# A hybrid encoder step: moving two sets of loads to ScalarE's queue and fixing the order of some products on TensorE

## The chip, the core and the metric

The kernel runs on one core of a Trainium2 chip. A core has five engines that run side by side, each with its own stream of instructions: TensorE multiplies matrices (PE in the profile, PEld for its loads of the stationary operand), VectorE (DVE) and GpSimd (POOL) work elementwise, ScalarE (ACT) computes functions and copies, and SyncE (SP) issues transfers. A transfer (DMA) can be issued from the stream of SP or of ScalarE; the profile names these queues q1 and q10. An engine takes its instructions in the order of its stream: one that must wait holds up all that stand behind it on that engine.

The metric is the device time of one execution in microseconds (us).

## The reference, cut to what matters

The reference computes one inference step of a two-layer encoder, for 2048 prompt tokens and 32 sampled tokens (2080 rows, model width 1024), all in float32.

Layer A is a gated delta rule with 8 heads of 128. The input is multiplied with a weight matrix of 4096 columns (and 16 for the gates). The columns of q, k and v pass a short causal convolution; then, in blocks, a state S per head is read and updated:

```python
decay = jnp.exp(jnp.where(incl, gcum[..., :, None] - gcum[..., None, :], -jnp.inf))
lower = jnp.where(strict, jnp.einsum('nbhik,nbhjk->nbhij', kbeta, kc) * decay, 0.0)
...
v_new = ui - jnp.einsum('bhck,bhkv->bhcv', wi, s)
o = jnp.einsum('bhck,bhkv->bhcv', qd, s) + jnp.einsum('bhij,bhjv->bhiv', ai, v_new)
s = s * gl[..., None, None] + jnp.einsum('bhck,bhcv->bhkv', kd, v_new)
```

The output o is normalized, weighed with a gate z, multiplied with output weights, added to the input and layer-normalized: this is h. From h come the shared keys and values, the queries and the gates of layer B, which is attention over a sliding window, again with output weights and a layer norm.

## The kernel before, in words

Products in float32 are made of three products of rounded parts: each operand is split into a high part (hi, a cast on ScalarE) and the rest (lo, a subtraction), and hi·hi, hi·lo and lo·hi are summed in PSUM. Tokens are taken in five blocks of 416 for projections and in 17 tiles of 128 (the last one holds the 32 sampled tokens) elsewhere. The kernel runs in stages:

1. **Projection** (class P1, `qkv`). For each of 24 columns of 128 outputs, weights are loaded (L46) and split (L53, L54), multiplied with the five blocks (`project`, L77 to L79), copied from PSUM into a row R by ScalarE (L258), convolved (L198 on ScalarE, three sums at L200 on VectorE), passed through tanh (L203) and stored. From column 7 on, one part of the output weights per column is loaded, split and stored again (`split_out_weights`, L1033 to L1036), in a buffer of the tag that tanh uses as well. From column 16 on, `decays` (L220) makes four or five decay matrices E per column: it loads cumulated gates, broadcast over 128 partitions (L231), adds a mask on VectorE (L239), takes the exponential on ScalarE (L243) and stores E (L244). E has three buffers; the load is made two steps ahead of its use. All of this is free for the planner: the framework simulates the program and sends each instruction when it is ready in the simulation, the earlier in the program the sooner.
2. **Gates z** of the first three blocks, beside first inverses.
3. **Delta stage** (class Delta, `run`). Seventeen chunks (the sampled one first) pass through a software pipeline. The string ORDER has 91 steps with offsets; each of the iterations i goes through all of them, for chunk i + offset. The engines TensorE, VectorE and ScalarE keep this written order here (`manual_schedule`); SP and GpSimd do not. In an iteration, `Lk` loads k, `G0` and `G1` multiply it (L627), `tv` transposes v (L741), `sp` and `SU` update the state, `oa` makes o, `sq`, `X`, `R` and `OSC` normalize it, and `otr`, `z`, `st` transpose it (L848), weigh it (L852) and store it (L855). From iteration OPEN = 11 on, the left part of the memory is free, and a function `side` is called after the steps 30 and 60: each call takes a step of `load_whole_weights`, two loads of 512 KB, high and low part (L1045, L1046), eight in all. From the ninth call on, the tables of the layer norm are loaded. From the last two iterations on, `second.give(0.45)` after each step with products fills in a group of output products (`OutNorm.tile`, L1070 to L1072, six products each). After the loop come the sampled tokens' last transposes, with 2 us of filling after each half.
4. **Output A** (class O1). What is left of the output products runs through `second.rest()`, in written order on TensorE and VectorE. Each tile is normalized (to L1148), stored, transposed (L1175), copied and stored again as hT.
5. **Layer B** (class P2, then Attention). `open_left` (called at L1661) loads the blocks 2 to 4 of hT and splits them (L68, L69); gate 1 is multiplied with the blocks 0 and 1 (L1662), then the gates 0 and 1 with the blocks 2 to 4, then values, keys, queries and attention. None of it has a written order.

Of the kernel before, what the change touches and what calls it, by code (L numbers as in the profile page):

```python
# [10 lines left out]
F32 = mybir.dt.float32  # L11
# [23 lines left out]
def new_pool(tc, es, name, bufs=1, space=None, side=None):  # L35
    kw = {"reuse_waits": "tile"}
    if side is not None:
        kw["side"] = side
    if space is not None:
        kw["space"] = space  # L40
    return es.enter_context(tc.tile_pool(name=name, bufs=bufs, **kw))
# [49 lines left out]
def drain(gen):  # L91
    for _ in gen:
        pass


class P1:
# [123 lines left out]
    def decays(self):  # L220

        nc, G, T = self.nc, self.G, self.T
        nm = self.one.tile([128, 128], F32, tag="triu", name="nm")
        nc.sync.dma_start(nm[:], self.I["nm"])
        todo = [(t, q) for t in (NTT - 1, *range(NTT - 1)) for q in range(2)]

        def load(m):
            t, q = todo[m]
            n, hs = min(128, NT - t * 128), slice(q * 4, q * 4 + 4)
            E = self.one.tile([128, 4, 128], F32, tag=("parts", "sel", "gtmp")[m % 3], name="E")  # L230
            nc.sync.dma_start(E[:, :, :n], T["gcum"][t, hs, :n].partition_broadcast(128))  # L231
            return E, t, n, hs

        ahead = [load(0), load(1)]
        for m in range(len(todo)):
            E, t, n, hs = ahead.pop(0)
            if m + 2 < len(todo):
                ahead.append(load(m + 2))
            nc.vector.tensor_tensor(out=E[:n, :, :n], in0=E[:n, :, :n],  # L239
                                    in1=nm[:n, :n].unsqueeze(1).to_broadcast([n, 4, n]), op=ALU.add)  # L240
            for j in range(4):
                h = hs.start + j
                nc.scalar.activation(E[:n, j, :n], E[:n, j, :n], AF.Exp, bias=G["ngc"][:n, t, h:h + 1])  # L243
            nc.scalar.dma_start(T["E"][t, :n, hs, :n], E[:n, :, :n])  # L244
            yield
# [291 lines left out]
class Delta:  # L537
# [365 lines left out]
    def run(self, chunks, S, gate, second, side, done):  # L903


        order = [(t[:t.index("+")], int(t[t.index("+") + 1:])) for t in self.ORDER.split()]
        steps, last = self.steps(), len(chunks) - 1
        for c, ch in enumerate(chunks):
            ch.S, ch.last = (self.S if ch.pool is None else S), ch.pool is not None or c == last
        gate.plan(order, self.FIRST + 2, self.WHOLE)  # L910
        gate.begin()
        for i in range(self.FIRST, last + 4):
            if i == self.OPEN:
                gate.finish()
                side(None)
            for p, (name, off) in enumerate(order):
                c = i + off
                if name in gate.STEPS:
                    m = c + gate.shift
                    gate.step(name, m)  # L920
                elif 0 <= c <= last and self.wanted(chunks[c], name):
                    steps[name](chunks[c])
                    if i >= last - 1 and name in self.WORK:
                        second.give(0.45)
                    if name == "st1":
                        done(chunks[c])
                if i >= self.OPEN and p in (len(order) // 3, 2 * len(order) // 3):
                    side(True)
            if i == last - 3 or i == last - 2:
                next(second.gen)  # L930
        c0 = chunks[0]
        c0.o = self.four.tile([128, 8, 128], F32, tag="gb", name="os", bufs=1)
        self.nc.sync.dma_start(c0.o[:NS], self.T["o"][:, :, :])
        self.load(c0, "z")
        for q in range(2):
            self.back(c0, q)
            self.gated(c0, q)
            self.store(c0, q)
            second.give(2.0)
        done(c0)  # L940

    def sampled(self, pool):
# [97 lines left out]
def load_whole_weights(nc, pool, kept):  # L1040

    hi, lo = (pool.tile([128, KC, D], F32R, tag=n, name=n) for n in ("wo_hi", "wo_lo"))
    yield hi, lo
    for k in range(KC):
        nc.sync.dma_start(hi[:, k, :].bitcast(F32), kept[0, k])  # L1045
        nc.sync.dma_start(lo[:, k, :].bitcast(F32), kept[1, k])  # L1046
        yield


# [542 lines left out]
def program(tc, I, O, T, G):  # L1592
    nc = tc.nc
    left, right, mid = ExitStack(), ExitStack(), ExitStack()
    p1 = P1(tc, left, right, mid, I, O, T, G)
    p1.qkv()
    mid.close()
    zp = new_pool(tc, left, "p1_z", 2, side="left")
    chunks = [Chunk(NP, NS)] + [Chunk(t * 128, 128) for t in range(16)]
    chunks[0].pool = zp  # L1600
    ahead = Ahead(tc, mid, left, I, O, T, G).inverses(chunks[:2])
    next(ahead)
    w = p1.first_gate(nc.gpsimd)
    z = p1.z((0, 1, 2), zp, ("zth", "z"), p1.ps, nc.gpsimd, w)
    with tc.manual_schedule(engines={mybir.EngineType.PE, mybir.EngineType.DVE}):
        for _ in range(28):
            next(z)
        for i, _ in enumerate(ahead):
            if i < 8 or i % 2:
                next(z, None)  # L1610
        drain(z)
    w = p1.first_gate(nc.gpsimd)
    raw = p1.late_raw(zp, 1)
    mid.close()
    right.close()
    delta = Delta(tc, right, I, O, T, G)
    S = delta.sampled(zp)
    sent = set()
    o1 = []

    def side(o):
        if o is None:
            left.close()
            o1.append(O1(tc, left, I, O, T, G))
        else:
            next(o1[0].on.rest, None)
            if o1[0].steps == 8:
                o1[0].on.tabs = o1[0].on.tables()
            o1[0].steps += 1

    def outputs():
        tiles = [(t * 128, t * 128, min(128, NT - t * 128)) for t in range(NTT)]
        yield from o1[0].tiles(tiles, lambda t: t[0] in sent, more)

    def more(i):
        if i == 0:
            p2[0].load_right()
            for j in range(2):
                p2[0].slab(j, nc.gpsimd)
        else:  # L1640
            yield from p2[0].gate(0, (i - 1,), p2[0].ps)

    p2 = []
    second = Filler(outputs())

    def done(ch):
        sent.add(ch.t0)

    ET = mybir.EngineType
    with tc.manual_schedule(engines={ET.PE, ET.DVE, ET.Activation}):  # L1650
        delta.run(chunks, S, LateGate(p1, zp, w, raw), second, side, done)
    right.close()
    hp = new_pool(tc, right, "o1_hT", 1, side="right")
    o1[0].room = lambda: hp.tile([128, KC, 128], F32, tag="hT", name="hT")
    p2.append(P2(tc, right, I, O, T))
    o1[0].bank = p2[0].ps
    with tc.manual_schedule(engines={ET.PE, ET.DVE}):
        second.rest()
    left.close()
    p2 = p2[0]  # L1660
    p2.open_left(left)  # L1661
    drain(p2.gate(1, (0, 1), p2.ps))  # L1662
    for b in (2, 3, 4):
        for i in (0, 1):
            drain(p2.gate(i, (b,), p2.ps))
    p2.values()
    p2.rotated()
    for i in (2, 3):
        p2.slab(i, nc.gpsimd)
        drain(p2.gate(i, range(NB), p2.ps))  # L1670
    late = range(4, 8)
    for i in late:
        p2.slab(i, nc.gpsimd)
        drain(p2.gate(i, (2, 3, 4), p2.ps))
    left.close()
    att = Attention(tc, left, I, O, T, G)
    att.load_kv(12, 18)
    order = list(range(14, 32)) + list(range(14))
    for i in late:
        p2.slab(i, nc.vector)  # L1680
        drain(p2.gate(i, (0, 1), p2.right_ps))
        att.chunk(order.pop(0))
        if i == late[0]:
            att.load_kv(18, 32)
    right.close()
    att.open_right(right)
    att.load_kv(0, 12)
    for n in order:
        for _ in range(2):
            next(att.rest, None)  # L1690
        att.chunk(n)
        if n == order[-2]:
            att.sample()
            att.flush(2)
        elif n % 2 == 1 and n != order[-1]:
            att.flush(3 if n < 24 and n > 13 else 2)
    att.flush(0)
    left.close()
    right.close()
# [138 lines left out]
```

## Time and profile before

| | us |
|---|---|
| three runs | 2221.84, 2222.75, 2215.28 (median 2221.84) |
| the profiled execution | 2216.86 |
| its span, from the first to the last instruction | 2215.1 |
| TensorE busy in it | 2150.1 |
| ScalarE busy | 901.1 |
| VectorE busy | 1379.1 |

All rows of the trace are from the profiled execution, in us from the start of its span; it took 1.8 us more than its span. A row of the timeline gives the start, the duration, the engine (SPq or ACTq for an issue of a transfer), the line, the instruction, what it writes and reads, the shape and, in brackets, how long the engine stood idle before it and what ended the wait. A row of waits gives who waited for whom, the sum, how often, and the longest. A row of windows gives a stretch, its length, the busy time of each engine with its number of instructions, the clock granted to TensorE as a share of full speed, the share of time that the 16 DMA engines were busy, and the GB/s that they moved. By their position in the trace, the stages are: the projection up to about 600, the delta stage up to about 1170, output A up to about 1355, layer B from there.

### The profile page before, as it was taken

The page shows a single profiled execution, that of the slowest core. Times are in us where ns is not written, and L with a number is a line of the kernel's source. Part 1 is how long each engine was busy: PE and PEld are TensorE (multiplying, and loading weights), DVE is VectorE, ACT ScalarE, POOL GpSimd, SP SyncE. Part 2 cuts the span into 40 slices and gives each one's busy share as a digit, 9 for nine tenths or more (in the row PEclk, how much of TensorE's full clock was granted, in tenths as well). Part 3 has the DMA queues.
Part 4 walks back from the last instruction along what each step waited for, and adds up shares of the span by engine and source line. Part 5 has one row for each costly group of instructions (what it writes and reads, how often), then busy time and mean ns, then how long its engine had stood idle before and what let it go on. Part 6 is the DMA issues. An engine that isn't in the chain of part 4 may idle for free.

```text
span 2215.1 us, 36944 instructions
## 1 busy us (share of the span) xinstructions
PE 2150.1 (97%) x13690; PEld 1980.3 (89%) x13690; DVE 1379.1 (62%) x2701; ACT 901.1 (41%) x2274; POOL 826.3 (37%) x1201
## 2 busy tenths in 40 slices
PE   8999999999899999996989999999999999999998
PEld 6999999999899999996977887999999987778885
DVE  3676666665567688885866886224543235668775
ACT  4444444456522566665641213222111245544442
POOL 1422223212212377776630201035442124555564
PEclk9999999999999999998999999999999999999999
DMA  5223333357655454448425764355212287233321
GB/s 196 68 61 90 99 111 106 97 170 223 192 157 157 145 161 160 152 157 324 160 85 184 231 196 125 125 197 187 83 66 79 73 196 264 77 93 98 96 72 53
DMA packets 268116, 308.29 MB, mean 139 GB/s; under 512 B 79728, under 2 KB 198832, under 8 KB 267664
## 3 DMA queue, kind: packets, MB, share of 16 engines
q1 hardware_dynamic: 253664, 285.42, 41.2%
q10 hardware_dynamic: 14272, 20.51, 2.7%
q8 instruction: 108, 1.77, 0.3%
q14 instruction: 72, 0.59, 0.1%
HBM read 189.63 MB, written 116.60 MB: 138 GB/s over the span
## 4 chain that ended last, share of the span: by engine, by line
PE 83%; DMA 7%; DVE 4%; POOL 2%; ACT 2%; issue 1%; SPq 0%; ACTq 0%; DVEq 0%; POOLq 0%
PE ps L77 14%; PE ps L79 14%; PE ps L78 14%; PE po L1070 5%; PE po L1072 5%; PE po L1071 5%; PE ot L1562 4%; DMA E<-s_gcum 2%; PE S L1541 2%; PE tr L1556 2%; DMA s_E<-E 1%; PE g L627 1%; PE gq L754 1%; PE sp L769 1%; PE ks L769 1%
## 5 line engine op out<-in xcount | busy, mean ns | idle before, releaser
L77 PE MATMUL ps<-act_hi,w_hi 128*128 128x416 f32 x2000 | 707.7, 355 | 5.9 <-ACT R L258 2.4
L79 PE MATMUL ps<-act_hi,w_lo 128*128 128x416 f32 x2000 | 706.5, 354 | 4.3 <-POOL w_lo L54 2.1
L78 PE MATMUL ps<-act_lo,w_hi 128*128 128x416 f32 x2000 | 703.2, 352 | 3.5 <-DVE act_lo L69 3.5
L77 PEld LDWEIGHTS ps<-act_hi,w_hi 128*128 128x128 f32 x2000 | 377.4, 189 | 12.8 <-ACT act_hi L68 3.7
L79 PEld LDWEIGHTS ps<-act_hi,w_lo 128*128 128x128 f32 x2000 | 376.8, 188 | 10.5 <-POOL w_lo L54 3.1
L78 PEld LDWEIGHTS ps<-act_lo,w_hi 128*128 128x128 f32 x2000 | 377.0, 188 | 9.7 <-DVE act_lo L69 5.3
L54 POOL TENSOR_TENSOR w_lo<-w_raw,w_hi 128x1024 fp32r<-128x1024 f32 x44 | 117.7, 2675 | 473.4 <-ACT w_hi L53 446.2
L200 DVE SCALAR_TENSOR_TENSOR y<-R,convw,y 128x2083 f32<-128x2083 f32 x72 | 181.8, 2526 | 38.7 <-POOL convo L194 22.5
L661 POOL TENSOR_TENSOR tm<-L,Tt 128x60 f32<-128x60 f32 (+19 forms) x375 | 130.3, 347 | 116.6 <-DVE tm L661 48.0
L1549 POOL TENSOR_TENSOR P<-P,sm 128x384 f32<-128x384 f32 (+2 forms) x128 | 100.6, 808 | 169.7 <-DVE sm L1427 101.2
L663 POOL TENSOR_TENSOR Tt<-Tt,tm 128x60 f32<-128x60 f32 (+19 forms) x375 | 143.8, 383 | 29.4
L1423 ACT ACTIVATE P<-S,nm 128x192 f32<-128x192 f32 (+3 forms) x260 | 104.8, 419 | 90.5 <-DVE nm L1416 43.8
L258 ACT COPY R<-ps 128x416 f32<-128x416 f32 (+1 forms) x144 | 60.7, 444 | 123.8 <-PE ps L79 105.3
L1070 PE MATMUL po<-wo_hi,g_hi 128*128 128x512 f32 x256 | 104.6, 408 | 0.0
L1072 PE MATMUL po<-wo_hi,g_lo 128*128 128x512 f32 x256 | 101.2, 395 | 0.5 <-DVE g_lo L1113 0.5
L1071 PE MATMUL po<-wo_lo,g_hi 128*128 128x512 f32 x256 | 100.9, 394 | 0.0
L1267 POOL TENSOR_TENSOR rs<-rs,sin 128x416 f32<-128x416 f32 x50 | 70.7, 1414 | 78.1 <-DVE rs L1266 72.3
L53 ACT CAST w_hi<-w_raw 128x1024 fp32r<-128x1024 f32 x48 | 50.4, 1050 | 119.5 <-PE ps L78 82.7
L1562 PE MATMUL ot<-pt,vd 128*128 128x256 f32 x372 | 97.1, 387 | 1.6 <-ACT pt L1558 1.1
L1070 PE MATMUL po<-wo,g_hi 128*128 128x512 f32 x224 | 92.9, 415 | 0.0
L1352 DVE SCALAR_TENSOR_TENSOR za<-zs,za 128x416 f32<-128x416 f32 x40 | 33.0, 826 | 93.3 <-ACT za L1351 93.2
L1072 PE MATMUL po<-wo,g_lo 128*128 128x512 f32 x224 | 90.1, 402 | 0.0
(301 smaller groups left out, 4073.6 us busy)
## 6 DMA issues: line engine op xcount, KB each, us to landing
w_raw<-in_w_in SPq DMA_DIRECT2D x40, 512.0 KB
w_raw<-in_b_w_in SPq DMA_DIRECT2D x20, 512.0 KB
k<-s_k SPq DMA_DIRECT2D x17, 512.0 KB
E<-s_E SPq DMA_DIRECT2D x17, 512.0 KB
s_bz<-za SPq DMA_DIRECT2D x40, 208.0 KB
s_bq<-ra SPq DMA_DIRECT2D x40, 208.0 KB
s_q<-y SPq DMA_DIRECT2D x8, 1024.0 KB
s_wo<-wo_parts SPq DMA_DIRECT2D x16, 512.0 KB
```

Of the source, the lines that this page charges most:

```text
L54: sub.tensor_tensor(out=lo[:], in0=raw[:], in1=hi[:], op=ALU.subtract)
L77: nc.tensor.matmul(ps, hi[:, k, :], xh[:, k, :], start=(k == 0), stop=False)
L78: nc.tensor.matmul(ps, hi[:, k, :], xl[:, k, :], start=False, stop=False)
L79: nc.tensor.matmul(ps, lo[:, k, :], xh[:, k, :], start=False, stop=(k == KC - 1))
L200: nc.vector.scalar_tensor_tensor(out=y[:], in0=R[:, j:j + W], scalar=self.convw[:, i, j:j + 1], in1=y[:], op0=ALU.mult, op1=ALU.add)
L661: P.tensor_tensor(out=tm[:n, i0 - k:, :w], in0=L[:n, i0:, j:j + 1].to_broadcast(sh), in1=Tt[:n, j:j + 1, :w].to_broadcast(sh), op=ALU.mult)
L663: P.tensor_tensor(out=Tt[:n, i0:, :w], in0=Tt[:n, i0:, :w], in1=tm[:n, i0 - k:, :w], op=ALU.subtract)
L1070: nc.tensor.matmul(ps[:n], ghi[:, k, :n], w[0][:, k, cs], start=a, stop=False)
L1071: nc.tensor.matmul(ps[:n], ghi[:, k, :n], w[1][:, k, cs], start=False, stop=False)
L1072: nc.tensor.matmul(ps[:n], glo[:, k, :n], w[0][:, k, cs], start=False, stop=z)
L1423: nc.scalar.activation(P[u], src, AF.Exp, bias=nm[:, u:u + 1], scale=1.0, accum_out=sm[:, u:u + 1])
L1562: nc.tensor.matmul(ot[:, p], self.vd[:, kc0 + j, p, :], pt[:, 2 * j:2 * j + 2, :], start=(j == 0), stop=(j == nj - 1))
```

## The change

It has four parts.

1. The loads of the output weights (L1045, L1046) are issued from ScalarE instead of SP, and `load_whole_weights` gives a step back after each single load. `side` is called in each iteration from OPEN on at the positions p with p % 18 = 10, that is 10, 28, 46, 64 and 82 of 91. The tables follow at the seventeenth call.
2. The loads of decays (L231) are issued from ScalarE, one step ahead instead of two.
3. The sampled tokens' last transposes move from behind the loop into a function `first_end`, which is called after the step `oa1` of the last chunk, with 2 us of filling ahead of the loads and 3 us behind them; the filling between the halves is gone.
4. `open_left` and the two blocks of gate 1 keep their written order on TensorE.

```diff
-            nc.sync.dma_start(E[:, :, :n], T["gcum"][t, hs, :n].partition_broadcast(128))
+            nc.scalar.dma_start(E[:, :, :n], T["gcum"][t, hs, :n].partition_broadcast(128))
...
-        ahead = [load(0), load(1)]
+        ahead = load(0)
         for m in range(len(todo)):
-            E, t, n, hs = ahead.pop(0)
-            if m + 2 < len(todo):
-                ahead.append(load(m + 2))
+            E, t, n, hs = ahead
+            if m + 1 < len(todo):
+                ahead = load(m + 1)
...
+                    if c == last and name == "oa1":
+                        self.first_end(chunks[0], second, done)
                     if name == "st1":
                         done(chunks[c])
-                if i >= self.OPEN and p in (len(order) // 3, 2 * len(order) // 3):
+                if i >= self.OPEN and p % (len(order) // 5) == 10:
                     side(True)
...
-        c0 = chunks[0]
+
+    def first_end(self, c0, second, done):
+        second.give(2.0)
         c0.o = self.four.tile([128, 8, 128], F32, tag="gb", name="os", bufs=1)
         self.nc.sync.dma_start(c0.o[:NS], self.T["o"][:, :, :])
         self.load(c0, "z")
+        second.give(3.0)
         for q in range(2):
             self.back(c0, q)
             self.gated(c0, q)
             self.store(c0, q)
-            second.give(2.0)
         done(c0)
...
     for k in range(KC):
-        nc.sync.dma_start(hi[:, k, :].bitcast(F32), kept[0, k])
-        nc.sync.dma_start(lo[:, k, :].bitcast(F32), kept[1, k])
+        nc.scalar.dma_start(hi[:, k, :].bitcast(F32), kept[0, k])
+        yield
+        nc.scalar.dma_start(lo[:, k, :].bitcast(F32), kept[1, k])
         yield
...
-            if o1[0].steps == 8:
+            if o1[0].steps == 16:
...
-    p2.open_left(left)
-    drain(p2.gate(1, (0, 1), p2.ps))
+    with tc.manual_schedule(engines={ET.PE}):
+        p2.open_left(left)
+        drain(p2.gate(1, (0, 1), p2.ps))
```

## The prediction

> **What bounds the kernel now.** I read the busy times first, then the shares of the chain that ended last, then what TensorE waited for.
>
> ```profile
> PE 2150.1 (97%) x13690; PEld 1980.3 (89%) x13690; DVE 1379.1 (62%) x2701; ACT 901.1 (41%) x2274; POOL 826.3 (37%) x1201
> ...
> PE 83%; DMA 7%; DVE 4%; POOL 2%; ACT 2%; issue 1%; SPq 0%; ACTq 0%; DVEq 0%; POOLq 0%
> ```
>
> TensorE is busy for 97% of the span and holds 83% of the last chain. The change takes no product away, so it can only give back TensorE's gaps and the slow clock after them. The waits of TensorE, longest first:
>
> ```profile
> PE g L627 <- DMA k<-s_k: 12.2, 1, 12.2
> ...
> PE vtr L741 <- DMA v<-s_v: 6.2, 1, 6.2
> PE otr L848 <- DVE o L839: 4.3, 1, 4.3
> PE ps L78 <- DVE act_lo L69: 3.5, 5, 1.9
> ...
> PE ps L77 <- ACT R L258: 2.4, 1, 2.4
> PE ps L77 <- ACT act_hi L68: 2.2, 3, 1.6
> PE ps L79 <- POOL w_lo L54: 2.1, 1, 2.1
> ```
>
> Four places, and the change has a part at each: two DMA waits in the delta stage (18.4 us), the end of the projection (R, w_lo), the end of the delta stage (otr), and the start of the second gates (act_lo, act_hi: 5.7).
>
> **Part 1: output weights on ScalarE's queue (L1045, L1046).** The busy times by stretch, one iteration of the delta loop or half a disturbed one each (PE, PEld, DVE, ACT, POOL, granted clock, DMA share, GB/s):
>
> ```profile
> 969.00:990.40 21.40, 21.40 (x245) 20.48 (x243) 17.82 (x48) 15.16 (x49) 14.33 (x42) 1.00 0.48 158
> ...
> 1011.86:1033.00 21.14, 18.18 (x222) 17.43 (x220) 20.25 (x50) 14.07 (x46) 17.62 (x46) 0.98 0.97 357
> 1033.00:1052.33 19.33, 3.97 (x29) 3.67 (x29) 0.12 (x1) 2.03 (x6) 6.32 (x20) 0.59 1.00 393
> 1052.33:1074.50 22.17, 22.17 (x248) 21.65 (x248) 17.98 (x47) 14.33 (x48) 10.79 (x32) 0.91 0.45 158
> ```
>
> An ordinary iteration moves 158 GB/s x 21.4 us = 3.4 MB at half load. In the disturbed one the DMA engines are full for 40 us and TensorE does almost nothing in the second half. Why, the rows of SP's queue show (first and last of the 16 weight loads, then loads of k):
>
> ```profile
> 1012.25 1.04 SPq L1045 DMA_DIRECT2D wo_hi<-s_wo  x1
> ...
> 1035.42 0.32 SPq L1046 DMA_DIRECT2D wo_lo<-s_wo  x1
> ...
> 1043.21 0.32 SPq L598 DMA_DIRECT2D k<-s_k  x1
> ```
>
> ```profile
> 1069.13 0.32 SPq L598 DMA_DIRECT2D k<-s_k  x1
> ```
>
> The code asks for two pairs per iteration over four iterations, but SP is not under the written order, and the planner sent all 16 (8.4 MB) within 23 us. The loads of v and k queue behind them. The blocks g that wait for k start here:
>
> ```profile
> 1011.86 2.05 PE L627 MATMUL g<-k 128*128 128x128 f32 x16
> ...
> 1052.33 3.76 PE L627 MATMUL g<-k 128*128 128x128 f32 x16 [12.16 <-DMA k<-s_k]
> ...
> 1074.52 2.05 PE L627 MATMUL g<-k 128*128 128x128 f32 x16
> ...
> 1095.96 2.05 PE L627 MATMUL g<-k 128*128 128x128 f32 x16
> ```
>
> From g to g: 40.5 us disturbed, 22.2 the next (slow clock), 21.4 undisturbed: 19.1 + 0.7 = 19.8 us lost. After the change the loads stand in ScalarE's stream, which is in written order inside the loop, one each at positions 10, 28, 46, 64 and 82 of 91: 5 x 0.52 = 2.6 MB per iteration, over 3.2 iterations. Then an iteration moves 3.4 + 2.6 = 6.0 MB, 15.3 us at the 393 GB/s of the full stretch: it fits in 21.4. The first is tighter. SP still has g, two r and the two tables (five loads of 0.52 MB in the list of DMA issues) free to go early: 8.6 MB, 21.9 us. So k, issued 5.4 us ahead of its use in the ordinary row (1069.13 to 1074.52) and landed 9.1 us after issue in the full one, can still come up to 3.7 us late, three times: 0 to 11.1. I take 2.8, near the light end, because only the first of the three iterations is full. ScalarE has room: five issues at 0.33 us (SP's rows of one load have 0.32 and 0.33) are 1.7 us beside 15.2 busy of 21.4. If that cover were gone they would cost 3.2 x 1.7 = 5.4 us. **Term: -17 us** (bounds -19.8 and -3.3, the last with 11.1 for k and 5.4 for issues).
>
> The Trainium skill, "DMA: Bandwidth & Descriptors", speaks against a gain here: its section "Issuing engines are not separate DMA queues" and its rules for kernel authors say that spreading loads over engines only saves the issuing sequencer's time, since all share the same 16 DMA engines. By that alone the bytes would be as late as now; its section "Queues, rings and completion order" adds that each DMA engine takes turns between rings, by which k would share turns with one weight load and not stand behind six. The full stretch (share 1.00) agrees with the shared engines; no row here shows the turns.
>
> **Part 2: decay matrices (L231) on ScalarE's queue, one ahead.** Slices at the end of the projection:
>
> ```profile
> 443.00:498.40 55.40, 55.40 (x296) 55.03 (x295) 34.33 (x39) 28.90 (x67) 9.38 (x12) 1.00 0.52 170
> 498.40:553.80 55.40, 55.40 (x296) 55.04 (x295) 28.43 (x22) 33.64 (x77) 11.62 (x13) 1.00 0.72 223
> 553.80:609.20 55.40, 49.14 (x236) 47.10 (x235) 31.87 (x19) 28.75 (x57) 12.41 (x13) 0.91 0.65 192
> ```
>
> 236 products where a full slice holds 296: 60/296 x 55.4 = 11.2 us lost, part of it clock. ScalarE is half idle, yet late with the cast of the next weights:
>
> ```profile
> 420.93 1.05 ACT L53 CAST w_hi<-w_raw 128x1024 fp32r<-128x1024 f32 x1 [3.34 <-PE ps L78]
> ...
> 581.61 0.62 ACT L1034 CAST wo_parts<-wo_parts 128x512 fp32r<-128x512 f32 x1 [6.84 <-DMA s_E<-E]
> 582.13 1.04 ACT L53 CAST w_hi<-w_raw 128x1024 fp32r<-128x1024 f32 x1
> ```
>
> Six columns took 161 us, 26.9 each, against 120 products x 0.188 (55.4/295) = 22.5 on TensorE: the lead of two weight buffers is eaten at 4.4 us per column, and the last column stalls. The loop that is too long: wo_parts is loaded into the buffer that y's tanh has just left, its cast holds ScalarE, then y's scaling, three sums on VectorE with decay adds between, tanh, and again. What ScalarE takes over, and what VectorE may be rid of:
>
> ```profile
> SPq L231 <- DMA s_E<-E: 68.0, 24, 10.2
> ```
>
> ```profile
> DVE E L239 <- DMA E<-s_gcum: 63.2, 19, 8.9
> ```
>
> ```profile
> 498.77 0.69 DVE L239 TENSOR_TENSOR E<-E,nm 128x512 f32<-128x512 f32 x1 [0.17 <-DMA E<-s_gcum]
> ```
>
> Gain: the E loads no longer stand on SP's queue behind the 1 MB store of y, so the four adds (0.69 us each) can fall before y's sums, up to 2.8 us per column. Cost: 34 issues x 0.33 us = 11 us over eight columns, and the wait for E's store, which now stops ScalarE: behind it stand the casts of w_hi, the copies of R that free PSUM, tanh, so TensorE. With one load ahead the awaited store is one unit older, so the 68 us is an upper end. Between a gain of 11.2 (the whole stall) and the rival below, the two sums of waits are about equal, so I take little. **Term: -3 us.**
>
> **Part 3: sampled transposes ahead.** Now, at the loop's end:
>
> ```profile
> 1158.85 0.48 PE L1070 MATMUL po<-wo_hi,g_hi 128*128 128x512 f32 x1
> ...
> 1164.76 1.32 PE L848 MATMUL otr<-ident,o 128*128 128x128 f32 x8 [4.28 <-DVE o L839]
> 1166.19 0.63 PE L848 MATMUL otr<-ident,os 32*128 32x32 f32 x4
> ```
>
> ```profile
> 1163.00:1218.40 55.40, 53.53 (x245) 43.55 (x246) 38.00 (x96) 9.14 (x11) 4.79 (x2) 0.94 0.59 184
> ```
>
> Lost: 4.3 idle and (1 - 0.94) x 55.4 = 3.3 of clock. The change puts 5 us of output products (four groups of six) and the sampled transposes ahead of the last chunk's. That would fill the gap, but VectorE is in written order too: the sampled z now stands ahead of the last S update, of X, the root and o.
>
> ```profile
> 1158.24 1.12 DVE L817 SCALAR_TENSOR_TENSOR Sp<-Sp,t_egl,sp 128x128 f32<-128x128 f32 x4 [0.95 <-PE sp L769]
> 1161.06 0.17 DVE L830 SCALAR_TENSOR_TENSOR Xo<-Xo,t_eq 128x8 f32<-128x8 f32 x1 [1.70 <-ACT vn L826]
> ...
> 1163.48 1.22 DVE L839 TENSOR_TENSOR o<-o,ro_y 128x1024 f32<-128x1024 f32 x1
> ```
>
> TensorE reaches the sampled transposes after five groups (1.36 us each, six products at the 0.227 that L1128 reckons with): 1158.9 + 6.8 = 1165.7; VectorE is held until then, and X to o takes 3.6 us (1161.06 to 1164.70), the S update 1.1: o is late by about 5 us again. The gap is moved, not filled. **Term: +1 us** (-7.6 to +6: the whole loss gone, or a second gap of its size less the clock).
>
> **Part 4: fixed gate order.** The last h is normalized by 1364.8, its transposes come later:
>
> ```profile
> 1360.34 0.35 PE L79 MATMUL ps<-act_hi,w_lo 128*128 128x416 f32 x1
> ...
> 1368.36 0.43 PE L1175 MATMUL ps<-ident,r 32*128 32x32 f32 x4
> ```
>
> ```profile
> 1364.08 0.74 DVE L1148 SCALAR_TENSOR_TENSOR r<-r,ln_y,ln_b 32x512 f32<-32x512 f32 x1
> ```
>
> The planner had moved products of gate 1 in between. Held to the written order, TensorE would stand 1360.5 to 1364.8, 4.3 us, and the activations would start 3.5 us earlier, off the 5.7 us of waits for them. With up to 3.3 us of slow clock as in part 3: -1.4 to +7.6, and 0 if the planner's order stays. **Term: +1.5 us.**
>
> **Sum.** -17 - 3 + 1 + 1.5 = -17.5. The profiled execution took 2216.86 us (span 2215.1 and 1.8 around it): 2199.4. The median shown, 2221.84, lies 5.0 above it (the three runs from 2215.28 to 2222.75), which gives 2204.3. I forecast 2202, between the two.
>
> **The rivals.**
> 1. *Everything closes.* All of parts 1 to 3 is given back: 19.8 + 11.2 + 7.6 = 38.6, so about 2183 from the median. For it: each loss is a wait for a transfer or an order. Against: the same VectorE order (part 3), and ScalarE still waits for wo_parts.
> 2. *Contention stays.* The weights and the early SP loads together still make k late, 3 x 3.7 + 5.4 = 16.5 us back: part 1 gives 3, the sum is about -4, 2218. For it: 357 to 393 GB/s are needed in the first iteration. Against: half load in the others. That the loads go out in one burst all the same (the change not doing what it says) ends here too; ScalarE's written order speaks against it.
> 3. *Slower: ScalarE becomes the bound of the projection.* If half of the 68 us of store waits lands in the loop, each of eight columns is 4.3 us longer; seven hand it on: 30 us more stall, -14.5 without the gain of part 2, together +15: 2237. It turns the sign from 14.5 / 7 = 2.1 us of added wait per column on. For it: copies of R and casts stand behind a waiting load. Against: the older store, and ScalarE's 45% idle time.
>
> By the Trainium skill, "TensorE: Matmul & The Clock Gate" (part 1), the clock falls after about 3.4 us of idle; here a stage with gaps of 2.4 and 2.1 us already shows 0.91, so I count clock for short gaps too.
>
> **How the numbers follow.** Chances: the forecast 0.56 (2192 to 2212), everything closes 0.16, contention 0.17, slower 0.11. About 0.3% (6.7 us) is what a measurement of this kernel can tell: faster means under 2215.2. Faster: 0.56 + 0.16 + 0.04 of contention = 0.76; same 0.13; slower 0.11. The range leaves out the slower rival and the better half of the first: 2187 to 2220.
>
> **What would show it.** Right: the waits for k and v together under 6 us, weight loads on ScalarE's queue some 4 us apart, no stretch of 40 us at full DMA share, over 250 products in the slice before 609. Part 3: os ahead of otr, with a wait for o still above 3 us. Part 4: a wait of the last transposes for r of 4 us. Wrong: a wait of TensorE for R or w_lo that grows in earlier columns (rival 3), or k late in each of three iterations (rival 2).

## The result and the profile after

The changed kernel takes 2212.20 us (median of 17 runs, 2207.82 to 2216.88), the kernel before 2218.27 us in 17 runs beside it (2214.47 to 2222.75). The ratio is 0.9971, with a 95% interval from 0.9962 to 0.9979: 6 us, or 0.3%, faster. The span of the profiled execution fell from 2215.1 to 2208.4 us, by 6.7. The forecast was 17.5 us less than the profiled execution, and 2202 us.

The busy times of the changed kernel look as before (TensorE 2151.5 us, 97% of the span); it is in the waits of TensorE (who waited for whom, sum, times, longest) that the change shows:

```profile
PE ps L77 <- ACT R L258: 6.1, 2, 3.2
PE otr L848 <- DVE o L839: 5.7, 1, 5.7
PE g L627 <- DMA k<-s_k: 4.2, 1, 4.2
...
PE ps L78 <- DVE act_lo L69: 2.5, 4, 1.3
...
PE vtr L741 <- DMA v<-s_v: 2.0, 1, 2.0
...
PE ps L77 <- ACT act_hi L68: 1.8, 2, 1.0
```

The waits for k and v fell from 18.4 to 6.2 us. The wait for o grew from 4.3 to 5.7, and the wait for R, the end of the projection, from 2.4 to 6.1. The slice there, which held 236 products before, now holds 219:

```profile
553.80:609.20 55.40, 45.30 (x219) 43.07 (x217) 25.10 (x18) 31.02 (x64) 11.26 (x11) 0.94 0.64 200
```

How much each part brought is read from blocks that both traces have, the products g in the timeline of the changed kernel:

```profile
1016.59 2.05 PE L627 MATMUL g<-k 128*128 128x128 f32 x16
1044.32 3.75 PE L627 MATMUL g<-k 128*128 128x128 f32 x16 [4.22 <-DMA k<-s_k]
1067.49 2.02 PE L627 MATMUL g<-k 128*128 128x128 f32 x16
1088.91 2.05 PE L627 MATMUL g<-k 128*128 128x128 f32 x16
```

The first of them stood at 1011.86 before. It now starts **4.7 us later**, and ahead of it only part 2 acts. The last stood at 1095.96: over these three iterations the changed kernel takes 72.3 us where the one before took 84.1, so **part 1 brought 11.8**. Behind them hardly anything moves. The last transposes of output A, which stood at 1368.36 before, show that:

```profile
1361.78 0.43 PE L1180 MATMUL ps<-ident,r 32*128 32x32 f32 x4
```

That is 6.6 us earlier, where the last g was 7.1 earlier: parts 3 and 4 together cost 0.5 up to here, and the end comes 6.7 earlier. The sum of the terms is -11.8 + 4.7 + 0.5 = -6.6.

What is left of part 1's loss: the stretches of the first full iteration and the next (columns as before: PE, PEld, DVE, ACT, POOL, granted clock, DMA share, GB/s).

```profile
1016.59:1030.00 13.41, 12.93 (x137) 12.24 (x136) 12.86 (x30) 8.83 (x30) 11.14 (x30) 1.00 0.96 330
1030.00:1044.32 14.32, 8.12 (x116) 7.66 (x115) 7.81 (x21) 7.38 (x23) 11.81 (x33) 0.97 1.00 389
1044.32:1067.49 23.17, 23.17 (x248) 22.61 (x249) 18.24 (x47) 14.32 (x48) 11.99 (x36) 0.87 0.66 232
```

The DMA engines are full for 28 us instead of 40, and in the iteration behind the waits TensorE's clock is at 0.87. The first six weight loads now go out three to seven us apart, in 23.4 us (the first and the last of them are shown), but SP sends the loads of output A in that same iteration:

```profile
1014.79 0.33 ACTq L1049 DMA_DIRECT2D wo_hi<-s_wo  x1
...
1038.18 0.35 ACTq L1051 DMA_DIRECT2D wo_lo<-s_wo  x1
```

```profile
1017.04 2.20 SPq L1105 DMA_DIRECT2D g<-s_g  x1
1019.58 0.33 SPq L1058 DMA_DIRECT2D ln_g<-in_a_ln_g  x1
1020.01 0.38 SPq L1059 DMA_DIRECT2D ln_b<-in_a_ln_b  x1
1020.45 1.63 SPq L1110 DMA_DIRECT2D r<-in_x  x2
...
1036.53 0.32 SPq L598 DMA_DIRECT2D k<-s_k  x1
```

The block g that needs this k starts at 1044.32, 7.8 us after the issue.

### The profile page after: what moved, and what is told of

Its sections match the earlier page's. It is cut to its first block, busy times and chain, and to the rows that moved or that the text cites. A ratio compares the mean times of both kernels' runs of the same rounds, so it can differ in the third digit from the quotient of the medians.

```text
span 2208.4 us, 36899 instructions
## 1 busy us (share of the span) xinstructions
PE 2151.5 (97%) x13690; PEld 1982.6 (90%) x13690; DVE 1373.8 (62%) x2701; ACT 900.9 (41%) x2274; POOL 825.7 (37%) x1201
## 4 chain that ended last, share of the span: by engine, by line
PE 65%; DMA 6%; DVE 3%; POOL 2%; ACT 1%; issue 1%; ACTq 0%; SPq 0%; DVEq 0%; POOLq 0%
PE ps L77 9%; PE ps L79 8%; PE ps L78 8%; PE po L1075 5%; PE po L1077 5%; PE po L1076 5%; PE ot L1567 4%; PE S L1546 2%; PE tr L1561 2%; DMA wo_parts<-in_a_w_out 1%; DMA E<-s_gcum 1%; PE g L627 1%; PE gq L754 1%; PE sp L769 1%; PE ks L769 1%; PE vp L769 1%
## 5 line engine op out<-in xcount | busy, mean ns | idle before, releaser
L79 PE MATMUL ps<-act_hi,w_lo 128*128 128x416 f32 x2000 | 707.0, 354 | 3.3 <-POOL w_lo L301 1.8
L79 PEld LDWEIGHTS ps<-act_hi,w_lo 128*128 128x128 f32 x2000 | 377.4, 189 | 8.9 <-POOL w_lo L301 2.1
L661 POOL TENSOR_TENSOR tm<-L,Tt 128x60 f32<-128x60 f32 (+19 forms) x375 | 130.4, 348 | 104.6 <-issue 40.2
```

Source lines behind the costliest of these rows:

```text
L79: nc.tensor.matmul(ps, lo[:, k, :], xh[:, k, :], start=False, stop=(k == KC - 1))
L661: P.tensor_tensor(out=tm[:n, i0 - k:, :w], in0=L[:n, i0:, j:j + 1].to_broadcast(sh), in1=Tt[:n, j:j + 1, :w].to_broadcast(sh), op=ALU.mult)
```

## The experiments

Theory: part 1 works as forecast but SP's early loads still crowd it; part 2 costs, since ScalarE is held by the loads it now issues; part 3 moves a gap that VectorE's written order makes; part 4 does nothing. The rivals stand with each run. "Projection" is the time from the tanh (L203) of column 15 to that of the last column, in the profiled execution; in the change and in e10, the kernel with E on GpSimd, these are

```profile
410.28 1.95 ACT L203 ACTIVATE th<-y 128x2083 f32<-128x2083 f32 x1 [2.33 <-DVE y L200]
...
616.74 1.95 ACT L203 ACTIVATE th<-y 128x2083 f32<-128x2083 f32 x1 [7.36 <-DVE y L200]
```

```profile
410.26 1.95 ACT L203 ACTIVATE th<-y 128x2083 f32<-128x2083 f32 x1 [2.35 <-DVE y L200]
...
605.15 1.95 ACT L203 ACTIVATE th<-y 128x2083 f32<-128x2083 f32 x1 [7.36 <-DVE y L200]
```

In the seven kernels here that leave that stage as it was before (loads of E on SP, two ahead), it lies between 199.7 and 203.0, so differences under 3 us say little. "Three iterations" is the time from g of iteration 11 to g of iteration 14, 64.3 if nothing is lost (three times 21.42). "Output A" is the time from g of iteration 14 to the first of the last transposes of 32 columns. These three are from one execution of each kernel, the medians from 4 to 6 runs (17 for the first two).

| kernel | median us | ratio to before, 95% | projection | three iterations | output A |
|---|---|---|---|---|---|
| before | 2218.27 | 1 | 201.6 | 84.1 | 272.4 |
| the change | 2212.20 | 0.9971 (0.9962 to 0.9979) | 206.5 | 72.3 | 272.9 |
| e1: E on SP, two ahead | 2205.80 | 0.9946 (0.9933 to 0.9959) | 199.9 | 69.9 | 271.9 |
| e2: E on ScalarE, two ahead | 2208.16 | 0.9962 (0.9949 to 0.9975) | 203.6 | 71.9 | 273.0 |
| e3: E on SP, one ahead | 2205.48 | 0.9950 (0.9935 to 0.9964) | 202.5 | 69.8 | 272.0 |
| e5: e1, early loads in written order | 2202.55 | 0.9939 (0.9926 to 0.9953) | 200.9 | 66.6 | 272.3 |
| e6: e5, first_end behind OSC | 2198.83 | 0.9913 (0.9899 to 0.9928) | 200.9 | 68.2 | 269.4 |
| e7: e5, four weight loads per iteration | 2202.24 | 0.9926 (0.9913 to 0.9938) | 199.7 | 64.6 | 274.4 |
| e8: e5 without part 4 | 2203.64 | 0.9929 (0.9915 to 0.9942) | 203.0 | 68.5 | 272.5 |
| e10: e5, E on GpSimd, two ahead | 2198.40 | 0.9910 (0.9895 to 0.9926) | 194.9 | 67.2 | 273.0 |
| f3: e5, E on GpSimd, one ahead | 2197.85 | 0.9910 (0.9897 to 0.9923) | 195.3 | 68.5 | 272.8 |
| f4: e5 without part 3 | 2202.11 | 0.9928 (0.9915 to 0.9941) | 202.1 | 67.7 | 273.4 |
| f5: e10, y stored twice, same place | 2208.52 | 0.9959 (0.9945 to 0.9973) | 211.8 | 66.8 | 272.2 |
| f6: e10, y stored twice, two places | 2204.60 | 0.9943 (0.9929 to 0.9956) | 197.3 | 66.3 | 272.9 |
| f1: e6 and e10 together | 2190.20 | 0.9875 (0.9862 to 0.9887) | 195.4 | 66.1 | 268.1 |
| f7: f1 and e7 together | 2188.86 | 0.9878 (0.9863 to 0.9893) | 195.8 | 66.2 | 268.1 |

### Part 2: which queue, how deep

e1 undoes part 2; e2 and e3 undo one half of it each.

```diff
-            nc.scalar.dma_start(E[:, :, :n], T["gcum"][t, hs, :n].partition_broadcast(128))
+            nc.sync.dma_start(E[:, :, :n], T["gcum"][t, hs, :n].partition_broadcast(128))   # e1, e3
...
-        ahead = load(0)
+        ahead = [load(0), load(1)]   # e1, e2, with the loop of before
```

> The change with its part 2 undone: the decay matrices E are loaded from SP's queue again, two ahead. Theory (part 2 cost 4.7 us: block g of iteration 10 started at 990.44 before and at 995.17 after, and nothing else of the change acts ahead of it): g of iteration 10 back within 0.5 us of 990.4, the rest as after, so about 4.7 us less than the changed kernel, some 2207.5 against 2212.2. Rival (the 4.7 us come from elsewhere, for instance another order of the projection that the planner chose for the whole program): g stays near 995 and the time near 2212.

> The change, but the loads of E on ScalarE's queue two ahead, as they were on SP's. Theory Q (the queue costs: ScalarE is held by its waits for E and by the issues): g of iteration 10 stays at 995 or comes later, since the awaited store is the newer one; 2212 or up to 2 us more. Theory D (the depth costs: one ahead is too short): g comes back to 990.4, time about 2207.5.

> The change, but the loads of E on SP's queue, one ahead. Theory Q (the queue costs): g of iteration 10 back at about 990.4 and about 2207.5. Theory D (the depth costs): g near 995, about 2212; behind the 1 MB store of y with one load ahead VectorE would wait for E longer than the 9 us that it waits after the change.

e1 is 6.4 us under the change, with the projection back at 199.9 and g of iteration 10 at 988.7, 1.7 us earlier than expected: part 2 cost. e3, on SP with the shallow depth, is as fast as e1. So one ahead the queue costs, and on SP the depth does not. e2 falls between: 4.0 us under the change, where theory Q expected none, and 2.4 above e1. Its interval overlaps both, so two ahead the cost of ScalarE's queue is not shown, and on that queue the depth may matter a little. ScalarE's rows in the changed kernel show how it is held (ACTq is its issue of a transfer; the bracket is its idle time before the instruction):

```profile
486.27 3.26 ACTq L231 DMA_DIRECT2D E<-s_gcum  x2
489.66 1.95 ACT L203 ACTIVATE th<-y 128x2083 f32<-128x2083 f32 x1 [3.82 <-DMA E<-s_gcum]
...
496.65 1.21 ACTq L231 DMA_DIRECT2D E<-s_gcum  x1
497.95 1.14 ACTq L244 DMA_DIRECT2D s_E<-E  x1
499.13 0.51 ACT L258 COPY R<-ps 128x416 f32<-128x416 f32 x1 [3.61 <-issue]
499.54 1.05 ACT L53 CAST w_hi<-w_raw 128x1024 fp32r<-128x1024 f32 x1
```

ScalarE stands idle for 3.8 us ahead of tanh, and the view puts this down to a load of E. Behind the store of y (issued at 495.51) an issue takes 1.2 us instead of 0.33, and the copy of R and the cast of the next weights stand behind 3.6 us of issues.

To see whether the loads come sooner from another stream, e10 issues them from GpSimd, which can issue transfers too, and f3 does so one ahead, which in this stage differs from the change in the issuing engine alone.

```diff
+            nc.gpsimd.dma_start(E[:, :, :n], T["gcum"][t, hs, :n].partition_broadcast(128))   # e10, f3; f3 one ahead
```

> The kernel with the five early loads in written order (2202.55), with the loads of E issued from GpSimd's stream, two ahead: neither behind the store of y on SP's queue nor in ScalarE's stream. Theory H (a queue of their own brings the E loads no sooner, since they share the DMA engines with the 1 MB store; what part 2 cost was ScalarE being held): the projection as with SP, 2202.5 plus or minus 1.5, VectorE still waits for E. Rival (the queue does delay them, as the prediction had it, and the change only paid for it on ScalarE): VectorE's wait for E falls, the stall of the last columns shrinks, 3 us or more less, below 2199.5.

> The loads of E from GpSimd (2198.4 with two ahead), but one ahead as in the change. Against the change this moves the loads, with their waits for the store of E and their issues, from ScalarE to GpSimd, and nothing else of the projection. From the tanh of column 15 (L203, at 410) to that of the last column: 206.5 us after the change, 194.9 from GpSimd two ahead. Theory H (what part 2 cost was ScalarE being held, the depth matters little): below 197, time within 2 us of 2198.4. Theory D (one ahead is what costs): 199 or more, time 2202 or more.

The projection falls to 194.9 and 195.3: some 6 us below the loads on SP, and 11.2 below the change at the same depth. The slice that held 236 products before and 219 after the change holds 271 in e10:

```profile
553.80:609.20 55.40, 52.83 (x271) 51.66 (x270) 35.12 (x22) 31.60 (x62) 14.02 (x18) 0.97 0.55 175
```

Theory H had expected no gain over SP; that half of it fell, and the rival of e10 holds by the signs it named: VectorE waits less for E, the stall of the last columns shrinks, and the time is 4.2 us less. So SP's queue had cost time, as the prediction said, and ScalarE's cost more. Theory H's other half, that ScalarE's hold is what part 2 cost, fits f3 and the rows above. Every kernel is planned anew, so the order of the stage is not the same in each; but four kernels with the loads on GpSimd agree within 0.9 us. VectorE's waits for E over 440 to 620 are 63.2 us before, 58.0 in e5; in the change and in e10:

```profile
DVE E L239 <- DMA E<-s_gcum: 53.0, 14, 9.5
```

```profile
DVE E L239 <- DMA E<-s_gcum: 40.2, 13, 8.9
```

SP's stream, too, is freed: in e5 it waits 65.3 us for stores of E before it can load E anew, and ScalarE waits 24.8 us ahead of the casts of wo_parts, whose loads stand in the same stream; in e10 GpSimd takes over the waits for the stores (22.7 us), and 13.1 are left ahead of the casts. Which of the two, E or wo_parts, brings the 6 us is not separated.

Yet the longest wait of each column is much the same, wherever the loads are issued. Behind the store of y (SP, L206), the add that waits long (L239) comes after 9.5 us in the change (9.1 behind the next store):

```profile
551.42 0.38 SPq L206 DMA_DIRECT2D s_v<-y  x1
```

```profile
560.88 0.69 DVE L239 TENSOR_TENSOR E<-E,nm 128x512 f32<-128x512 f32 x1 [9.48 <-DMA E<-s_gcum]
```

and after 9.6 and 9.4 us in e10, from GpSimd:

```profile
541.35 0.38 SPq L206 DMA_DIRECT2D s_v<-y  x1
568.10 0.38 SPq L206 DMA_DIRECT2D s_v<-y  x1
```

```profile
550.92 1.09 DVE L239 TENSOR_TENSOR E<-E,nm 128x512 f32<-128x512 f32 x1 [7.17 <-DMA E<-s_gcum]
577.45 0.69 DVE L239 TENSOR_TENSOR E<-E,nm 128x512 f32<-128x512 f32 x1 [7.16 <-DMA E<-s_gcum]
```

In e5, from SP, it is much the same, 9.2 us:

```profile
547.57 0.37 SPq L206 DMA_DIRECT2D s_v<-y  x1
```

```profile
556.80 0.69 DVE L239 TENSOR_TENSOR E<-E,nm 128x512 f32<-128x512 f32 x1 [9.26 <-DMA E<-s_gcum]
```

So it was not the place on SP's queue alone that kept this E. The issues of the awaited loads say more. In e10 the first of them goes out 2.6 us behind the store:

```profile
543.93 0.54 POOL L231 DMA_DIRECT2D E<-s_gcum  x1 [3.90 <-DVE E L239]
```

It lands 7.0 us later, where the median of E's loads in that stage is 3.8; the second one goes out at 570.86, after GpSimd had stood idle for 4.4 us until a store of E had landed, and takes 6.6 us. In the change the awaited load goes out at 552.55, 1.1 us behind the store, and takes 8.3 us. So in these places the wait is made of an issue that comes only behind the store and of a landing that takes longer than the median. Two runs ask whether it is the bytes of the store. Both store y of the eight columns of v a second time.

```diff
+            if kind == 2:
+                nc.sync.dma_start(dst[0:NTT - 1, :, h, :].rearrange("t p k -> p t k"),       # f5; f6: T["y2"] instead of dst
+                                  y[:, 0:NP].rearrange("p (t k) -> p t k", k=128))
```

> The loads of E from GpSimd, two ahead (2198.4), and the 1 MB store of y of the eight columns of v done twice on SP's queue. Theory B (the E loads share the DMA engines with the store, whatever queue they stand on): VectorE's longest waits for E, 6 to 9 us in a column, grow by about the 2.7 us that 1 MB takes at 390 GB/s, and the columns with them, by up to 8 x 2.7 = 21 us in all; I expect 5 to 20 us more. Rival (the order on one queue is what counts, a load on a queue of its own passes the store): the waits stay, 2198 to 2200.

> As f5_store_twice, but the second 1 MB store of y goes to a scratch array of its own, so that it doesn't wait for the first and SP's queue is not held: only bytes are added beside the E loads on GpSimd (2198.4). Theory B (the E loads share the DMA engines with the store, on whatever queue): VectorE's longest wait for E in a column grows from 6.6 to 7.2 us to 9 or more, the projection from tanh to tanh by 5 us or more, the time to 2203 or more. Rival (in f5 it was SP's wait that cost, and E on a queue of its own passes the store): waits as in the kernel with one store, time 2198 to 2200.

f5 is 10.1 us longer, as theory B has it by the time, though its longest wait for E is 7.7 us and has not grown. But its second store waits for the first to land, so SP is held as well:

```profile
494.49 0.36 SPq L206 DMA_DIRECT2D s_v<-y  x1
500.38 0.36 SPq L209 DMA_DIRECT2D s_v<-y  x1
```

f6 takes that wait away and is still 6.2 us longer than e10 by the medians. Its projection is only 2.4 longer, but its g of iteration 10 starts 5.6 us later (989.18 against 983.61; the four kernels from GpSimd with one store lie within 0.9), so the loss falls ahead of that block. Its long-waiting add behind the two stores (L242 here, three lines further down) comes no later:

```profile
540.25 0.38 SPq L206 DMA_DIRECT2D s_v<-y  x1
540.68 1.93 SPq L209 DMA_DIRECT2D s_y<-y  x1
```

```profile
547.77 0.69 DVE L242 TENSOR_TENSOR E<-E,nm 128x512 f32<-128x512 f32 x1 [6.94 <-DMA E<-s_gcum]
```

7.5 us after the store, with twice the bytes. Neither expectation holds: the second store costs time, by more waits of 2 to 3 us (64.4 us of waits for E in all, against 40.2) and longer waits ahead of the casts of wo_parts (26.9 us against 13.1), but it does not lengthen the long wait. Whether a fourth buffer of E, which might let the load go out ahead of the store of y, shortens it was not tried.

### Part 1: what still crowds the first iteration

e5 takes e1 and issues the first load of g, the first two of r and the two tables from ScalarE's stream, where they keep their written place (short form of the edit):

```diff
-        self.nc.sync.dma_start(g[:, :, :n], src)
+        (self.nc.scalar if first_of_output_A else self.nc.sync).dma_start(g[:, :, :n], src)   # the same for r, twice
...
-    nc.sync.dma_start(gt[:], g.partition_broadcast(128))
+    nc.scalar.dma_start(gt[:], g.partition_broadcast(128))   # and bt; output A alone
```

e7 spreads the weights further, over four iterations:

```diff
-                if i >= self.OPEN and p % (len(order) // 5) == 10:
+                if i >= self.OPEN and p % (len(order) // 4) == 10:
```

> The first kernel of this list (E on SP, two ahead), and besides the first load of g, the first two of r and the two tables of output A from ScalarE's stream in written order, so that SP can't send these 2.6 MB in the first open iteration. Theory S (those loads share the full stretch with five weight loads, and that makes v and k late): the waits for v and k in iteration 12 (2.0 and 4.2 us after the change) under 2 us together, g of iteration 12 to iteration 11 back from 27.7 to about 22, the time some 5 to 6 us below the first of this list, near 2202. Rival W (the weight loads alone, five per iteration, fill the queues): waits and time as in the first of this list, or later ones in iterations 13 to 15, near 2207.

> The kernel with the five early loads in written order (2202.55), but four weight loads per iteration (positions 10, 32, 54 and 76) over four iterations, instead of five over three. Theory B (what is left of the loss, 2.3 us from the g of iteration 11 to the g of iteration 14, is the load of the queues by 2.6 MB per iteration beside the loop's own 3.4): the wait for k in iteration 12, 2.4 us, goes below 1, some 1 to 2.5 us less, about 2201. Rival (the wait comes from something else in that iteration, a load of k that is issued late): k waits as long, time 2202.5; or the last weights come late for the first output products, up to 3 us more.

e5 is 3.3 us faster than e1 by the medians, with overlapping intervals; three iterations take 66.6 instead of 69.9, the same 3.3. The other kernels bear it out: with SP's early loads (the change, e1, e2, e3) they take 69.8 to 72.3, and in the nine with these loads in written order and five weight loads per iteration 66.1 to 68.5; the means are 3.7 apart. The wait for v is gone, that for k, at 2.4 a little above the 2 expected, is:

```profile
1034.17 3.39 PE L627 MATMUL g<-k 128*128 128x128 f32 x16 [2.42 <-DMA k<-s_k]
```

So theory S holds for rather more than half of what e1 had left, 5.6 us. In e7 that wait is gone too and the three iterations are back at 64.6, but the time is that of e5: output A takes 2.1 us more. The stretch right behind the three iterations runs at a clock of 0.92 in e7 and at 1.00 in e5, and the wait for o is 0.5 us longer. The rows of e7 and of e5:

```profile
1075.47:1096.85 21.38, 19.82 (x225) 19.40 (x224) 16.55 (x45) 13.54 (x45) 17.31 (x53) 0.92 0.62 213
```

```profile
1077.62:1099.00 21.38, 19.87 (x236) 19.11 (x234) 16.95 (x46) 15.17 (x47) 17.39 (x52) 1.00 0.64 210
```

Why the clock fell there is not settled.

### Part 3: who makes the gap

VectorE's rows in the changed kernel at the loop's end:

```profile
1158.37 0.54 DVE L852 TENSOR_TENSOR z<-otr,z 128x128 f32<-128x128 f32 x2 [1.66 <-PE otr L848]
1158.83 1.11 DVE L817 SCALAR_TENSOR_TENSOR Sp<-Sp,t_egl,sp 128x128 f32<-128x128 f32 x4
1159.86 0.79 DVE L830 SCALAR_TENSOR_TENSOR Xo<-Xo,t_eq 128x8 f32<-128x8 f32 x1
...
1162.89 1.22 DVE L839 TENSOR_TENSOR o<-o,ro_y 128x1024 f32<-128x1024 f32 x1
```

The sampled z waits for TensorE's sampled transposes, and only behind it run the S update, X, the root and o. e6 keeps the filling and the sampled transposes ahead of the last chunk's on TensorE, but writes them behind o in VectorE's stream; f4 undoes part 3.

```diff
-                    if c == last and name == "oa1":
+                    if c == last and name == "OSC":   # e6
                         self.first_end(chunks[0], second, done)
```

> The kernel with the five early loads in written order (2202.55), and the call of first_end behind the step OSC of the last chunk instead of oa1: the same 5 us of filling and the sampled transposes still stand ahead of the last chunk's transposes on TensorE, but VectorE has X, the root and o in its stream before the filler's sums and the sampled z. Theory V (the gap is made by VectorE's written order: the sampled z waits for TensorE and holds X to o, which need some 4 us): the wait of otr for o falls from 5.3 us to under 1.5, 4 to 6 us less in all, about 2197.5. Rival (the filling itself is short, or the path from the last op over ScalarE's squares to o is as long as the filling): the wait stays over 4 us and the time near 2202.5.

> The kernel with the five early loads in written order (2202.55), with part 3 undone: the sampled tokens' last transposes behind the loop again, with 2 us of filling after each half. Theory (part 3 moved the gap and gained nothing, +0.5 us by the traces): the wait of otr for o back at about 4.3 us instead of 5.3, the time within 1.5 us of 2202.5. Rival (part 3 did gain, and something else took it back): 3 us or more longer.

f4 is at 2202.11 against 2202.55, its wait for o is 4.3 us, and output A takes 273.4 us against 272.3 in e5, inside the 271.9 to 274.4 of the kernels that keep part 3 as it was: no gain of part 3 can be told. Its row:

```profile
1150.94 1.97 PE L848 MATMUL otr<-ident,o 128*128 128x128 f32 x8 [4.27 <-DVE o L839]
```

e6 is 3.7 us faster than e5, a little less than expected, and the wait for o is gone. Output A takes 269.4, 2.9 less (f1 and f7, with the same edit, 268.1); of the 6.0 us by which the span of the profiled execution is shorter, 4.4 fall behind it in layer B, which the edit does not touch. In place of the wait for o stands a shorter one, for the sampled z:

```profile
1147.94 0.68 PE L848 MATMUL otr<-ident,os 32*128 32x32 f32 x8
1150.84 0.66 PE L848 MATMUL otr<-ident,o 128*128 128x128 f32 x4 [2.22 <-DVE z L852]
```

TensorE has the same products in the same order, and only what was written ahead of o on VectorE differs: theory V holds.

### Part 4, and the parts that gain together

e8 writes `open_left` and the two blocks of gate 1 without a written order again, as before. f1 joins e6 and e10; f7 joins f1 and e7.

> The kernel with the five early loads in written order (2202.55), with part 4 undone: no written order for open_left and the blocks of gate 1. Theory N (part 4 made no difference: the end of output A came 6.59 us earlier and the last transposes of 32 columns 6.58 us earlier after the change): within 1 us of 2202.5. Rival (part 4 gained by the waits for act_lo and act_hi, 5.7 us in all before and 4.3 after): 1.4 us or more longer.

> Both edits that gained, on top of the kernel with the five early loads in written order (2202.55): first_end behind OSC, and the loads of E from GpSimd, two ahead. If the two are independent, as their places 500 us apart in the trace suggest: 2202.55 - 3.7 - 4.2 = 2194.7. Rival (one hands its gain back, for instance to a later load or the clock): about 2198.

> The fastest so far (2190.2), with four weight loads per iteration over four iterations. With five per iteration its block g of iteration 12 still waited 2.0 us for k. Theory (the rest of part 1's loss is load on the queues): the wait goes, and since the loop's end no longer waits for VectorE, the gain is kept: some 2 us less, 2188. Rival (as in e7, where the wait went and the time stayed): 2190.

e8 is 1.1 us longer, with overlapping intervals and a projection that happens to be 2.1 longer; output A is 272.5 against 272.3: no effect that can be told. f1 takes 2190.20 us, 4.5 less than the sum of the two gains would give; both edits keep what they brought. It beats the kernel before by 1.25% (ratio 0.9875, 0.9862 to 0.9887), and the change too. Why it beats the sum is not shown. f7 can't be told from it; its block g still waits for k twice (2.9 us in all), so here four loads per iteration took nothing away, and what is left of part 1's loss, about 2 us, stays unexplained.

## Why the prediction was wrong: the sign held, the size did not

The kernel became faster, as forecast, but by 6.1 us, just under the 6.7 that the text took as what can be told. In the trace it is 6.6 us for 17.5: 5.2 of the difference lie in part 1 and 7.7 in part 2, and parts 3 and 4 give 2.0 back. By its number the result is nearest to rival 2 (contention, -4), but not by its mechanism: k came late in one iteration, not in three.

- **What bounds the kernel.** Right. What was gained or lost came from TensorE's waits and the slow clock behind them (it is busy for 2150.1 us before and 2151.5 after), and f1 is faster by narrowing three of the four places named.
- **Part 1, -17.** The mechanism was right (the first six loads some 4 us apart, no stretch of 40 us at full share), the size was not: -11.8, inside the bounds. The failed step is "I take 2.8, near the light end, because only the first of the three iterations is full". One full iteration was enough to lose 8.1: k came 4.2 us late, v, which the term does not have, 2.0, and then 23 us ran at a clock of 0.87, which cost 1.8. The waits for k and v are 6.2 us together, just over the 6 that were to show it right. The text had itself counted the five early loads of SP in that iteration; e5 shows them to be worth 3.3 of the 5.6 that e1, which has part 1 without part 2, still lost. By the Trainium skill, "DMA: Bandwidth & Descriptors", section "Issuing engines are not separate DMA queues", another issuing engine would have brought no more than issue time. Yet 11.8 us came; the trace shows that the loads now go out one at a time and later, of which that rule says nothing. No run issues them from SP in written order, so the share of the queue itself is not shown.
- **Part 2, -3.** Wrong in sign: +4.7 in the trace, and 6.4 by the medians of the change and e1. The failed step is the balance, "the two sums of waits are about equal, so I take little". The gain was there: off SP's queue, on GpSimd, the projection is some 6 us shorter, about half of the 11.2 that bounded it. The cost was taken too low: from ScalarE the same loads, one ahead, make the projection 11.2 us longer than from GpSimd (f3). The two make about +5, which is what the change shows; the sign of over 250 products in the slice before 609 failed with 219. The sums of waits could not tell this: SP's 68 us held transfers, and GpSimd waits 16 to 23 us for the same stores and the projection is shorter all the same, while on ScalarE the casts, the copies of R and tanh stand behind each issue. The reason given for the gain, that the adds can fall before y's sums, is not shown: the add that waits longest still comes some 9 us after the store from all three engines. Rival 3 had the mechanism, at nearly three times the price (30 us of stall for 11.2).
- **Part 3, +1.** Right, +0.5 with part 4, and for the reason given (e6, f4). The wait for o was forecast above 3 us and is 5.7.
- **Part 4, +1.5.** Nothing: the case "0 if the planner's order stays". Products of the second gates (L79) still run up to the last transposes, and no wait of these for r appears, where one of 4 us was the sign.
- **From trace to median.** The three runs shown had a median of 2221.84; over 17 runs it is 2218.27, from which the same sum gives 2200.8. The base did not make the miss.

## What to carry to other kernels

Before a load is moved to another engine, look at what stands behind it on that engine's stream: its wait and its issue hold everything, and an engine with idle time on average is not idle at that place. A sum of waits does not price this; the same loads cost time from ScalarE and gained some from GpSimd, whose own work (w_lo) TensorE did not come to wait for longer. The transfers that were under no written order here went out early, so five forgotten loads filled the stage that others were just moved out of. Work that is written ahead to fill a gap on one engine must not, in the stream of another, stand ahead of the chain that ends the gap.

## What the runs showed of the hardware

- An issue on ScalarE's queue took 0.33 us at most places, but 1.14 to 1.21 us behind the store of y (the rows at 496.65 and 497.95). The sum of the prediction had 0.33 throughout. GpSimd's issues of the same loads took 0.54 to 0.56 us, behind the store as well (in f6 0.54 us, half a us behind it).
- The 1 MB store of y took about 5.9 us until a second store to the same place could be issued (f5, 494.49 to 500.38).
- TensorE's clock stood at 0.87 over the 23 us after waits of 2.0 and 4.2 us, at 0.92 over the 22 us after a wait of 2.4 us in e5 (1034.17 to 1056.12), and at 0.92 in a stretch of e7 whose iterations before had no wait for k or v.
